# An encoder layer on one core: x split into tiles by block, w_out's tiles taking x's places one by one, and the last head's attention between the products

## The chip, the core and the metric

The kernel runs on one core of a Trainium2 chip. Its engines are TensorE (PE: matrix products, with a queue of its own for weight loads, PEld), VectorE (DVE), ScalarE (ACT), GpSimd (POOL) and SyncE (SP), which here issues every transfer. Each engine takes its instructions in a fixed order; one that waits holds up all behind it on that engine. The metric is device time in microseconds (us) of one execution, as the median of several runs; lower is better.

## What is computed

One layer of a bidirectional encoder runs over two requests, a prompt of 1024 tokens and a sample of 256, each with 16 learned meta tokens ahead:

```python
u = rms_norm(h, norm_w) @ w_in                      # 2048 -> 6656
qa, ka, va, za, qb, kb, vb, zb = split(u)           # heads of 128
ya = global_gqa(rope(norm(qa)), rope(norm(ka)), va) * silu(za)          # 8 heads, 2 kv heads
yb = neighbourhood_attention(norm(qb), norm(kb), vb, rpb) * silu(zb)    # 8 heads
out = h + concat(ya, yb) @ w_out                    # 2048 -> 2048; meta tokens dropped
```

Neighbourhood attention gives each token of a 64-wide grid the 16 meta tokens and a window of 8 x 16 tokens, with a relative bias. Inputs and outputs are 32-bit floats.

## The kernel before

**Precision.** A 32-bit product is made of three matmuls of a shorter format (fp32r): high x high, high x low, low x high. Each operand is split for that by a cast on ACT (L61, the high part) and a subtraction on DVE (L62, the low part). A split therefore costs one instruction on each of the two engines, and DVE's waits for ACT's.

**Projection.** `strips` (L176) makes u in 52 strips of 128 columns. Tokens are worked in two chunks: chunk 1 has 512 tokens (meta, sample, 240 of the prompt), chunk 2 the other 784 of the prompt in blocks of 512 and 272. A strip goes over the 2048 inputs in 4 parts of 4 tiles (WCH = 4); in each part over the blocks, and in each block over the 4 tiles, with the three matmuls at L210, L211 and L212. Weights come as raw tiles (wr, pool "raw") and are split into wh and wl (pool "w", four places each). `load_all_x` loads and splits x for chunk 2 into 16 tiles of 1584 columns, each with the parts of both blocks in it (XLAY). They lie where chunk 1's x tiles were, so a load waits until the last chunk-1 strip has passed the tiles that it covers; the loads go in an order (3, 4, 0, 1, 2, 5 ...) that follows these places.

**Attention.** The 8 global heads go first. The 8 neighbourhood heads are attended in 32 blocks, four to a head; block 4h+b is block b of head h. A block's steps in `attend_strip` (L416) are: scores on PE (L438, L272, L273), a maximum over DVE and POOL (L452, L455, L282, L284), exponentials, the meta tokens' weights Pm (L294), sums over POOL (L299, L301), the attention product on PE (L467, L470; its result is po), then y = product x gate / sum on DVE (L310, L311, L314, L318) and a write of y to device memory (yd, L319). Blocks 0 to 27 are spread between the late strips, which are the k, q, z and v strip of each neighbourhood head in turn, in the list at L836 to L843. The last head's tiles are loaded when block 27 is done (`load(7)`), and blocks 28 to 31 run at the beginning of the output products.

**Output products.** `outproj` (L979) does y @ w_out with 7 half-size products in place of 8, in passes 1, 2, 5, 6, 7, 3, 4. A pass has 5 token tiles t and 2 halves b of 512 columns: 10 steps, and 70 in all, counted here as steps 0 to 69. A step is 24 matmuls (8 tiles of k, three each; L940 to L942). Its operands are a y tile (`y_load`, `y_operand`: loaded from yd, in some passes combined with another, then split into yo, a pool of three) and 8 split w tiles (`w_load`, `w_operand`: raw tiles ww in the places of wh and wl, eight in all, split into wm, 16 places). Passes 1 and 2 read w_out itself, others sums of its quarters from device memory (td). yd[0] holds the global heads' y, yd[1] the neighbourhood heads' y, so that pass 1 needs no neighbourhood attention and pass 2 does. The pools "us", "wm" and "yo" open where the pool of x was, once that is closed behind the last strip.

**Order.** Up to step 10 a scheduler sets the order on each engine from the program's order and its own estimates, and moves loads ahead where places are free. From step 10 on, `in_order` holds each engine to the program's order. All transfers stand in one queue on SP: a load that waits for its place holds up the ones behind it.

## Time and profile before

| what | us |
|---|---|
| median of 3 runs | 2192.64 |
| lowest and highest of them | 2191.17, 2193.61 |
| the profiled execution's own time | 2193.63 |
| its span in the trace | 2191.8 |
| PE busy in the span | 2165.2 (99%) |
| DVE, ACT, POOL busy | 1646.2, 1124.4, 518.2 |
| PE's share of the chain that ended last | 94% |

The page of the profile lists busy time by engine, then the span in 40 slices with the granted clock of TensorE, the chain of waits that ended last, the costliest groups of instructions with the idle time before them, and the DMA issues. PE is busy nearly all the time, so the places to read are those where it is not: a listing of waits names each instruction that PE stood at and what ended the wait; a timeline of the stretch shows what ran around it; and busy time by stretches gives the granted clock (1.00 is full speed) and the share of the 16 DMA engines in use. A busy matmul at a lower clock is lost time too, though it counts as busy.

### The profile page before, as it was taken

How to read it: one execution, taken by the hardware profiler on the slowest of the kernel's cores; microseconds unless marked ns; L12 is line 12 of the kernel's file. 1: busy time of each engine (PE TensorE's matmuls, PEld its weight loads, DVE VectorE, ACT ScalarE, POOL GpSimd, SP SyncE). 2: the span in 40 equal slices, each digit the busy share in tenths (PEclk: the TensorE clock that was granted, in tenths of full speed). 3: DMA queues.
4: the chain of work that ended last, by engine and by line, in shares of the span. 5: the costliest groups of instructions: out<-in, count | busy, mean ns of one | idle time of the engine just before them, and what ended most of it. 6: DMA issues, size and time to landing. Idle time of an engine off the chain costs nothing.

```text
span 2191.8 us, 34025 instructions
## 1 busy us (share of the span) xinstructions
PE 2165.2 (99%) x11736; PEld 1881.7 (86%) x11736; DVE 1646.2 (75%) x2956; ACT 1124.4 (51%) x2259; POOL 518.2 (24%) x249
## 2 busy tenths in 40 slices
...
GB/s 297 221 196 229 280 307 303 345 275 264 129 220 143 106 108 116 106 107 143 104 111 116 98 122 188 167 139 137 133 123 134 95 235 113 221 190 125 218 228 113
DMA packets 262173, 383.82 MB, mean 175 GB/s; under 512 B 44880, under 2 KB 113136, under 8 KB 262000
## 3 DMA queue, kind: packets, MB, share of 16 engines
...
## 4 chain that ended last, share of the span: by engine, by line
PE 94%; DVE 2%; DMA 2%; ACT 1%; issue 1%; SPq 0%; POOL 0%; DVEq 0%; ACTq 0%; POOLq 0%
PE pp L210 21%; PE pp L211 21%; PE pp L212 21%; PE pq L942 6%; PE pq L941 6%; PE pq L940 6%; PE po L470 2%; PE sp L438 1%; PE sp L333 1%; PE sp L334 1%; PE sp L332 1%; PE po L374 1%; PE po L372 1%; PE po L373 1%; DMA ww<-in_w_out 0%
## 5 line engine op out<-in xcount | busy, mean ns | idle before, releaser
L210 PE MATMUL pp<-x,wh 128*128 128x512 f32 (+1 forms) x2496 | 892.4, 359 | 7.3 <-ACT wh L61 5.5
L211 PE MATMUL pp<-x,wh 128*128 128x512 f32 (+1 forms) x2496 | 888.6, 356 | 0.4 <-DVE x L159 0.4
L212 PE MATMUL pp<-x,wl 128*128 128x512 f32 (+1 forms) x2496 | 888.7, 356 | 0.0
L210 PEld LDWEIGHTS pp<-x,wh 128*128 128x128 f32 x2496 | 469.1, 188 | 71.6 <-ACT wh L61 7.0
L212 PEld LDWEIGHTS pp<-x,wl 128*128 128x128 f32 x2496 | 469.6, 188 | 60.9 <-DVE wl L62 0.7
L211 PEld LDWEIGHTS pp<-x,wh 128*128 128x128 f32 x2496 | 469.9, 188 | 59.9 <-DVE x L159 1.3
L220 POOL PARTITION_ALL_REDUCE m<-ms x78 | 225.8, 2895 | 378.2 <-ACT ms L218 333.3
L62 DVE TENSOR_TENSOR wl<-wr,wh 128x512 fp32r<-128x512 f32 (+1 forms) x290 | 213.1, 738 | 130.3 <-ACT wh L61 105.3
L61 ACT CAST wh<-wr 128x512 fp32r<-128x512 f32 (+1 forms) x290 | 174.9, 607 | 224.6 <-PE pp L211 206.7
L301 POOL PARTITION_ALL_REDUCE tot<-a x80 | 178.2, 2228 | 470.2 <-DVE a L299 455.1
L940 PE MATMUL pq<-wm,yo 128*128 128x512 f32 x560 | 222.0, 396 | 0.0
L941 PE MATMUL pq<-wm,yo 128*128 128x512 f32 x560 | 221.3, 395 | 0.0
L942 PE MATMUL pq<-wm,yo 128*128 128x512 f32 x560 | 221.0, 395 | 0.0
L284 POOL PARTITION_ALL_REDUCE ma<-m x80 | 104.6, 1307 | 423.3 <-DVE m L282 415.1
L942 PEld LDWEIGHTS pq<-wm,yo 128*128 128x128 f32 x560 | 105.5, 188 | 24.8 <-DVE yo L62 0.4
L941 PEld LDWEIGHTS pq<-wm,yo 128*128 128x128 f32 x560 | 105.6, 189 | 24.6
L940 PEld LDWEIGHTS pq<-wm,yo 128*128 128x128 f32 x560 | 105.8, 189 | 24.3
L336 ACT COPY S<-sp 128x512 f32<-128x512 f32 x136 | 78.4, 579 | 51.2 <-PE sp L334 38.9
L194 ACT CAST wh<-wr 128x512 fp32r<-128x512 f32 x132 | 81.1, 614 | 41.5 <-PE pp L211 41.4
L62 DVE TENSOR_TENSOR pl<-S,ph 128x512 fp32r<-128x512 f32 x136 | 97.9, 732 | 3.9 <-ACT ph L61 3.8
L352 DVE TENSOR_TENSOR S<-S,ma 128x512 f32<-128x512 f32 x136 | 97.1, 772 | 3.9 <-POOL ma L284 3.9
L61 ACT CAST ph<-S 128x512 fp32r<-128x512 f32 x136 | 83.2, 612 | 32.9 <-PE po L373 32.3
...
## 6 DMA issues: line engine op xcount, KB each, us to landing
wr<-in_w_in SPq DMA_DIRECT2D x414, 256.0 KB, 3.5
wld<-wl SPq DMA_DIRECT2D x132, 256.0 KB, 4.4
wl<-wld SPq DMA_DIRECT2D x132, 256.0 KB, 3.1
wq<-in_w_out SPq DMA_DIRECT2D x64, 256.0 KB, 5.2
td<-wq SPq DMA_DIRECT2D x64, 256.0 KB, 4.3
ww<-td SPq DMA_DIRECT2D x64, 256.0 KB, 4.9
yr<-yd SPq DMA_DIRECT2D x30, 512.0 KB, 5.4
ww<-in_w_out SPq DMA_DIRECT2D x48, 256.0 KB, 5.3
```

The lines of the kernel that those rows point to most:

```text
L61: self.hi = nc.scalar.copy(hi, full).ins
L62: return nc.vector.tensor_tensor(out=lo, in0=full, in1=hi.bitcast(F32), op=ALU.subtract).ins
L210: nc.tensor.matmul(p[:, :n], wh[:, k, :], xh[:, :n], start=first, stop=False)
L211: nc.tensor.matmul(p[:, :n], wh[:, k, :], xl[:, :n], start=False, stop=False)
L212: nc.tensor.matmul(p[:, :n], wl[:, k, :], xh[:, :n], start=False, stop=last)
L220: nc.gpsimd.partition_all_reduce(m2[:], ms[:], P, RED.add)
L284: nc.gpsimd.partition_all_reduce(ma[:], m1[:], P, RED.max)
L301: nc.gpsimd.partition_all_reduce(tot[:], a1[:], P, RED.add)
L352: nc.vector.tensor_tensor(out=s, in0=s, in1=mb, op=ALU.subtract)
L940: nc.tensor.matmul(ps[:], yh, wh, start=k == 0, stop=False)
L941: nc.tensor.matmul(ps[:], yh, wl, start=False, stop=False)
L942: nc.tensor.matmul(ps[:], yl, wh, start=False, stop=k == 7)
```

## The change

Six edits belong together.

1. `load_all_x` gives each of the 16 tiles of x two tiles: "xa" with the 512-token block, the same size and place as chunk 1's x tile, and "xb" (560 columns) with the 272-token block, in places of their own. The order of tiles is 0 to 15.
2. The pools of x stay open. w_out's raw tiles are loaded into places of "xb" (16), the split ones go into places of "xa" (16), each as the last strip has passed it. All 16 raw tiles of the first pass are asked for ahead of the products; of each later pass, four are asked for at each of the steps with t = 2 and t = 3.
3. y operands are made in the pool "w", as two halves of 4 k tiles each (yh in "wh", yl in "wl"). With four places of each, two y tiles are held where there were three.
4. Passes 2 and 4 load y through the pool "yr" like the other combined passes, once the attention has ended. Of the ten results that pass 1 keeps (U), eight lie in "us" and two in "raw".
5. The late strips of a head come in the order v, k, q, z (before: k, q, z, v).
6. `outproj` advances the last head's attention blocks only at steps 3 and on (`if 2 < n < 2 * NT`), so blocks 28 to 31 are asked for at steps 3 to 6 instead of 0 to 3.

```diff
@@ -30,8 +30,8 @@
 T1 = NMETA + NS + C1P
 T2 = NP - C1P
 NB = 512
-XLAY = ((0, 512, 512), (1024, 1312, 272))
-TX = 1584
+NT2 = 272
+NX = 560
 ALIGN = 128
 NH = 8
 EPS = 1e-6
@@ -145,14 +145,14 @@
 
 
         nc = self.nc
-        t = [self.x.tile([P, TX], F32R, tag="x", name="x", align_bytes=ALIGN) for _ in range(KT)]
-        for kt, i in enumerate((3, 4, 0, 1, 2, *range(5, KT))):
+        for kt in range(KT):
             w = self.nw[:, kt:kt + 1]
             self.xs[kt] = []
+            ta = self.x.tile([P, 2, NB], F32R, tag="xa", name="x", align_bytes=ALIGN)
+            tb = self.xb.tile([P, NX], F32R, tag="xb", name="xb", align_bytes=ALIGN)
             o = 0
-            for a, b, n in XLAY:
-                h, l = t[i][:, a:a + n], t[i][:, b:b + n]
-                r = l.bitcast(F32)
+            for h, l in ((ta[:, 0], ta[:, 1]), (tb[:, :NT2], tb[:, NX - NT2:])):
+                r, n = l.bitcast(F32), l.shape[1]
                 with self.tc.issue_after(self.early):
                     nc.sync.dma_start(r, self.x2d[kt][:, o:o + n])
                 nc.scalar.activation(h, r, AF.Copy, scale=w)
@@ -835,8 +835,8 @@
         kw, qw, kwb, qwb = (self.nqkw[:, i:i + 1] for i in (1, 0, 3, 2))
         late = []
         for h in range(NH):
-            late += [qk_late(KB + h, kwb, self.k2d[2 + h]), qk_late(QB_ + h, qwb, self.q2d[8 + h]),
-                     z_late(ZB + h, self.zd[8 + h]), v_rows_of(VB + h, 2 + h)]
+            late += [v_rows_of(VB + h, 2 + h), qk_late(KB + h, kwb, self.k2d[2 + h]), qk_late(QB_ + h, qwb, self.q2d[8 + h]),
+                     z_late(ZB + h, self.zd[8 + h])]
 
         def fill(n):
             for _ in range(min(n, len(late))):
@@ -884,42 +884,51 @@
             self.nc.sync.dma_start(r[:], self.yd[i][:, NT * h + t])
             return r[:]
 
-        if p in (1, 2, 4):
-            r = self.yo.tile([P, 2, 8, P], F32R, tag="yo", name="yo", align_bytes=ALIGN)
-            self.nc.sync.dma_start(r[:, 1].bitcast(F32), self.yd[p > 1][:, NT * (p == 4) + t])
-            return r
-        return [half(*x) for x in {7: [(0, 0), (0, 1)], 5: [(0, 1), (1, 1)], 6: [(0, 0)], 3: [(1, 0)]}[p]]
+        if self.yr is None:
+            los = [self.w.tile([P, WCH, P], F32R, tag="wl", name="yl") for _ in range(2)]
+            for i, l in enumerate(los):
+                self.nc.sync.dma_start(l[:].bitcast(F32), self.yd[p > 1][:, t, WCH * i:WCH * i + WCH])
+            return los
+        return [half(*x) for x in {7: [(0, 0), (0, 1)], 5: [(0, 1), (1, 1)], 6: [(0, 0)], 3: [(1, 0)], 2: [(1, 0)], 4: [(1, 1)]}[p]]
 
     def y_operand(self, p, t, r):
         nc = self.nc
-        if p in (1, 2, 4):
-            self.split(r[:, 0], r[:, 1], r[:, 1].bitcast(F32))
-            return r
-        if p == 7:
+        if len(r[0].shape) == 3 and r[0].shape[1] == WCH:
+            his, los, full = [], r, [l[:].bitcast(F32) for l in r]
+            for l, f in zip(los, full):
+                his.append(self.w.tile([P, WCH, P], F32R, tag="wh", name="yh"))
+                self.split(his[-1][:], l[:], f)
+            return his, los
+        if p in (2, 4):
+            v = r[0]
+        elif p == 7:
             v = r[0]
             nc.vector.tensor_tensor(out=v, in0=v, in1=r[1], op=ALU.subtract)
         else:
             v = self.ysum[t][:]
             a, b, op = {5: (r[0], r[-1], ALU.add), 6: (v, r[0], ALU.subtract), 3: (r[0], v, ALU.subtract)}[p]
             nc.vector.tensor_tensor(out=v, in0=a, in1=b, op=op)
-        o = self.yo.tile([P, 2, 8, P], F32R, tag="yo", name="yo", align_bytes=ALIGN)
-        self.split(o[:, 0], o[:, 1], v)
-        return o
+        his, los = [], []
+        for i in range(2):
+            his.append(self.w.tile([P, WCH, P], F32R, tag="wh", name="yh"))
+            los.append(self.w.tile([P, WCH, P], F32R, tag="wl", name="yl"))
+            self.split(his[i][:], los[i][:], v[:, WCH * i:WCH * i + WCH])
+        return his, los
 
     def w_load(self, p, j):
 
         b, k = divmod(j, 8)
         src = {1: (0, 0), 2: (8, 0), 3: (8, FH)}.get(p)
-        r = self.w.tile([P, FB], F32, tag=("wh", "wl")[j % 2], name="ww")
+        r = self.xb.tile([P, FB], F32, tag="xb", name="ww", align_bytes=ALIGN)[:]
         if src is None:
-            self.nc.sync.dma_start(r[:], self.td[p][:, k, FB * b:FB * b + FB])
+            self.nc.sync.dma_start(r, self.td[p][:, k, FB * b:FB * b + FB])
         else:
-            self.nc.sync.dma_start(r[:], self.io["w_out"][:, src[0] + k, src[1] + FB * b:][:, :FB])
+            self.nc.sync.dma_start(r, self.io["w_out"][:, src[0] + k, src[1] + FB * b:][:, :FB])
         return r
 
     def w_operand(self, r):
-        w = self.wm.tile([P, 2, FB], F32R, tag="wm", name="wm", align_bytes=ALIGN)
-        self.split(w[:, 0, :], w[:, 1, :], r[:])
+        w = self.x.tile([P, 2, FB], F32R, tag="xa", name="wm", align_bytes=ALIGN)
+        self.split(w[:, 0, :], w[:, 1, :], r)
         return w
 
     def x_load(self, p, t, b):
@@ -936,7 +945,7 @@
         ps = self.pq.tile([P, FB], F32, tag="pq", name="pq")
         for k in range(8):
             wh, wl = ws[k][:, 0, :], ws[k][:, 1, :]
-            yh, yl = y[:, 0, k, :], y[:, 1, k, :]
+            yh, yl = (a[k // WCH][:, k % WCH, :] for a in y)
             nc.tensor.matmul(ps[:], yh, wh, start=k == 0, stop=False)
             nc.tensor.matmul(ps[:], yh, wl, start=False, stop=False)
             nc.tensor.matmul(ps[:], yl, wh, start=False, stop=k == 7)
@@ -950,7 +959,7 @@
             nc.vector.tensor_tensor(out=out, in0=a, in1=b, op=op)
 
         if p == 1:
-            self.U[i] = self.us.tile([P, FB], F32, tag="u", name="u")
+            self.U[i] = (self.us if i < 8 else self.raw).tile([P, FB], F32, tag="u" if i < 8 else "raw", name="u")
             nc.scalar.copy(self.U[i][:], ps)
             return None
         if p == 5:
@@ -977,7 +986,7 @@
         self.nc.sync.dma_start(self.io["y"][:, NT * h + t, FH * c + FB * b:][:, :FB], o[:])
 
     def outproj(self, end_attention):
-        self.U, self.V = {}, {}
+        self.U, self.V, self.yr = {}, {}, None
         order = (1, 2, 5, 6, 7, 3, 4)
         N = 2 * NT * len(order)
 
@@ -1009,12 +1018,9 @@
                 ws[q, j] = self.w_operand(wr.pop((q, j)))
 
         make_y(0)
-        for j in range(8):
+        for j in range(16):
             load_w(0, j)
-        for j in range(16):
             make_w(0, j)
-            if j < 8:
-                load_w(0, 8 + j)
         traced = None
         for n in range(N):
             p, t, b = step(n)
@@ -1029,9 +1035,9 @@
             if n - 2 in out:
                 self.store(out.pop(n - 2), *step(n - 2))
             last = t == NT - 1
-            if t == NT - 2 and b == 0:
-                for j in range(8):
-                    load_w(q + 1, j)
+            if NT - 3 <= t < NT - 1:
+                for j in range(4):
+                    load_w(q + 1, 8 * (t - NT + 3) + 4 * b + j)
             if q:
                 for i in (n, n + 1, n + 2):
                     if i < N and i not in x:
@@ -1045,12 +1051,10 @@
             if last:
                 for k in range(8):
                     make_w(q + 1, 8 * b + k)
-                    if b == 0:
-                        load_w(q + 1, 8 + k)
             o = self.out_sums(p, 2 * t + b, ps, x.pop(n, None))
             if o:
                 out[n] = o
-            if n < 2 * NT:
+            if 2 < n < 2 * NT:
                 next(self.blocks, None)
             if traced:
                 traced = self.in_order(traced)
@@ -1104,18 +1108,16 @@
                     self.chunk1()
                 self.raw = raw
                 pool(es_x, "x", 16, side="right", **kw)
+                pool(es_x, "xb", 16, side="right", **kw)
                 pool(es_proj, "ev", 8, side="right", **kw)
                 for name, bufs in (("k", 1), ("v", 1), ("tab", 1), ("q", 1), ("z", 1), *work, ("y", 1), ("qf", 1)):
                     pool(es_attn, name, bufs, **kw)
                 self.chunk2()
                 es_proj.close()
-                es_x.close()
-                es_one.close()
                 es_pp.close()
                 pool(es_y, "pq", 4, space=PSUM, **kw)
 
-                for name, bufs in (("us", 2 * NT), ("wm", 16), ("yo", 3)):
-                    pool(es_late, name, bufs, side="right", **kw)
+                pool(es_late, "us", 8, side="right", **kw)
 
                 def end_attention():
                     es_attn.close()
@@ -1125,6 +1127,8 @@
 
                 self.outproj(end_attention)
                 es_late.close()
+                es_x.close()
+                es_one.close()
 
 
 def _grid(rows):
```

The order of the instructions moves with it. In the rows below, sp is a tile of scores, po a result of an attention product, pq a result of an output product, m1 a maximum, ww a raw and wm a split w tile; numbers behind a name tell tiles apart.

PE from the end of the last strip to the first output product, before:

```order
L212 MATMUL pp<-x,wl 128x272
L438 MATMUL sp<-qfull,kfull 128x128 x2
L272 MATMUL sp<-q,km 112x256
L273 MATMUL sp<-q,km 112x256
L438 MATMUL sp<-qfull,kfull 128x192 x2
L491 MATMUL tp<-ident,vt 128x128 x6
L491 MATMUL tp<-ident,vt 16x128
L438 MATMUL sp<-qfull,kfull 128x128 x2
L438 MATMUL sp<-qfull,kfull 128x192 x2
```

Two more groups of scores and block 27's product follow there, and then the first output product. In the changed kernel only the first of these groups (block 27's) stands behind the last strip, then step 0, and block 27's product stands in the middle of step 1:

```order
L951 MATMUL pq_20413<-wm_20353,yl_20286 128x512
L467 MATMUL po_20239<-Pm_270,vm3_271 128x256
L470 MATMUL po_20239<-S_20205,vw_19448 128x128 x2
L470 MATMUL po_20239<-S_20206,vw_19448 128x192 x2
L949 MATMUL pq_20413<-wm_20358,yh_20293 128x512
```

The transposes (tp) have moved between the strips; the scores of block 28 come after step 3, those of blocks 29, 30 and 31 each after one step more.

DVE around block 27's maximum (m1_20200 before, m1_20219 now), before:

```order
L452 TENSOR_TENSOR m1_20200<-S_20186,S_20187 128x256
L62 TENSOR_TENSOR q_20254<-qfull_20251,q_20254 128x1024
L62 TENSOR_TENSOR wm_20335<-ww_20298,wm_20335 128x512
L455 TENSOR_TENSOR m1_20200<-m1_20200,S_20187 128x128
L62 TENSOR_TENSOR wm_20338<-ww_20303,wm_20338 128x512
L62 TENSOR_TENSOR wm_20341<-ww_20308,wm_20341 128x512
L282 TENSOR_TENSOR m1_20200<-m1_20200,Sm_20192 16x256
```

and with the change:

```order
L62 TENSOR_TENSOR yl_20376<-yl_20376,yh_20380 128x512
L264 SCALAR_TENSOR_TENSOR za_20184<-z_20182,za_20184 128x512
L452 TENSOR_TENSOR m1_20219<-S_20205,S_20206 128x256
L318 SCALAR_TENSOR_TENSOR y_20055<-y_20055,r_20050 128x256
L62 TENSOR_TENSOR yl_20377<-yl_20377,yh_20383 128x512
L455 TENSOR_TENSOR m1_20219<-m1_20219,S_20206 128x128
L267 TENSOR_TENSOR zt_20181<-z_20182,za_20184 128x512
L259 TENSOR_TENSOR z_20193<-pp_20060,rb2_317 128x272
L282 TENSOR_TENSOR m1_20219<-m1_20219,Sm_20211 16x256
```

The splits between the maximum's parts were of w tiles and of head 7's q; now one is of the second half of y tile 1 (yl_20377). On SP that half is asked for here, behind the sixteenth w tile of pass 1 (ww_20371) and seven of pass 2:

```order
L926 DMA ww_20371<-in_w_out 128x512
L890 DMA yl_20376<-yd0_165 128x512
L926 DMA ww_20555<-in_w_out 128x512
L926 DMA ww_20557<-in_w_out 128x512
L926 DMA ww_20559<-in_w_out 128x512
L926 DMA ww_20561<-in_w_out 128x512
L926 DMA ww_20651<-in_w_out 128x512
L926 DMA ww_20653<-in_w_out 128x512
L926 DMA ww_20655<-in_w_out 128x512
L890 DMA yl_20377<-yd0_165 128x512
```

What moved: the y halves now stand among the w tiles of the next pass, one load each, where before a y tile was one load.

PE at the last attention product, block 31's, before (in step 6, pq_20757):

```order
L467 MATMUL po_20664<-Pm_270,vm3_271 128x256
L470 MATMUL po_20664<-S_20630,vw_20245 128x128 x2
L470 MATMUL po_20664<-S_20631,vw_20245 128x192 x2
L941 MATMUL pq_20757<-wm_20320,yo_20679 128x512
L942 MATMUL pq_20757<-wm_20320,yo_20679 128x512
```

and with the change (in step 11, pq_21056; step 12 is pq_21096):

```order
L470 MATMUL po_20818<-S_20784,vw_20264 128x128 x2
L470 MATMUL po_20818<-S_20785,vw_20264 128x192 x2
L949 MATMUL pq_21056<-wm_20969,yh_20926 128x512
L950 MATMUL pq_21056<-wm_20969,yh_20926 128x512
L951 MATMUL pq_21056<-wm_20969,yl_20920 128x512
L949 MATMUL pq_21056<-wm_20972,yh_20926 128x512
L950 MATMUL pq_21056<-wm_20972,yh_20926 128x512
L951 MATMUL pq_21056<-wm_20972,yl_20920 128x512
L949 MATMUL pq_21056<-wm_20975,yh_20926 128x512
L950 MATMUL pq_21056<-wm_20975,yh_20926 128x512
L951 MATMUL pq_21056<-wm_20975,yl_20920 128x512
L949 MATMUL pq_21096<-wm_20893,yh_21019 128x512
```

Its y goes to yd[1] and comes back as part of step 12's y tile (yh_21019, made of yr_21009); block 31's product has moved from five steps ahead of step 12 to nine matmuls ahead of it.

## The prediction

> **What bounds the kernel now.** I read the busy row of the page first, then busy time by stretches, then the list of what TensorE waits for, then TensorE's timeline over the one stage where it waits. The columns of the stretches are: start and end, length, busy time of PE, its weight loads, DVE, ACT and POOL (instructions in brackets), granted clock, DMA share, GB/s.
>
> ```profile
> span 2191.8 us, 34025 instructions
> PE 2165.2 (99%) x11736; PEld 1881.7 (86%) x11736; DVE 1646.2 (75%) x2956; ACT 1124.4 (51%) x2259; POOL 518.2 (24%) x249
> ...
> 600.00:610.00 10.00, 9.81 (x45) 7.68 (x43) 3.52 (x6) 3.02 (x8) 0.00 (x0) 1.00 0.38 119
> 610.00:620.00 10.00, 7.31 (x33) 4.88 (x34) 8.02 (x18) 7.78 (x20) 3.99 (x2) 1.00 0.82 250
> 620.00:630.00 10.00, 10.00 (x56) 8.76 (x57) 9.97 (x22) 9.74 (x21) 0.00 (x0) 1.00 0.97 314
> 1755.00:1765.00 10.00, 10.00 (x60) 8.98 (x59) 4.95 (x13) 2.94 (x7) 2.01 (x2) 1.00 0.53 167
> 1765.00:1790.00 25.00, 13.00 (x67) 11.52 (x66) 19.96 (x40) 16.18 (x32) 2.86 (x2) 0.73 0.87 306
> 1900.00:2000.00 100.00, 100.00 (x432) 81.09 (x431) 51.31 (x66) 32.78 (x51) 0.00 (x0) 1.00 0.49 169
> ```
>
> TensorE bounds the kernel, at 99% of the span, and the change removes no matmul. So only its idle time can move. In the products it runs 432 matmuls in 100 us, 0.2315 us each, so a step of 24 takes 5.56 us with nothing lost. Two places stand out: 610 to 620, where chunk 2 begins, and 1765 to 1790, between the last strip and the products, where PE works 13 us of 25 at a mean clock of 0.73.
>
> What it waits for from 1740 to the end (microseconds in total, times, longest), and the timeline of that place (start, duration, operation, and in brackets the idle time before it):
>
> ```profile
> PE sp L438 <- DMA qfull<-q2d: 4.0, 1, 4.0
> PE po L467 <- DVE Pm L294: 3.3, 1, 3.3
> PE sp L438 <- DVE S L443: 2.5, 1, 2.5
> PE tp L491 <- ACT vl L493: 2.2, 1, 2.2
> ```
>
> ```profile
> 1743.28 0.28 PE L467 MATMUL po<-Pm,vm 128*128 128x256 f32 x1
> ...
> 1744.36 0.53 PE L212 MATMUL pp<-x,wl 128*128 128x512 f32 x1
> ...
> 1748.30 0.61 PE L438 MATMUL sp<-qfull,kfull 128*128 128x128 f32 x4
> ...
> 1749.49 0.53 PE L210 MATMUL pp<-x,wh 128*128 128x512 f32 x1
> ...
> 1767.77 0.61 PE L438 MATMUL sp<-qfull,kfull 128*128 128x128 f32 x4
> ...
> 1771.90 0.55 PE L491 MATMUL tp<-ident,vt 128*128 128x128 f32 x3 [2.19 <-ACT vl L493]
> ...
> 1786.73 0.58 PE L467 MATMUL po<-Pm,vm 128*128 128x256 f32 x1 [3.29 <-DVE Pm L294]
> ...
> 1790.59 0.61 PE L438 MATMUL sp<-qfull,kfull 128*128 128x128 f32 x4
> ...
> 1791.27 0.40 PE L942 MATMUL pq<-wm,yo 128*128 128x512 f32 x1
> ```
>
> The last strip's work ends at 1767.77 and undisturbed products go on from 1791.27: 23.5 us. The work in between, at the full-clock prices of the same rows: three groups of scores at 1749.49 - 1748.30 = 1.19 (3.6), one attention product at 1744.36 - 1743.28 = 1.08, half a group at 1791.27 - 1790.59 = 0.68, four product matmuls 0.93, seven transposes about 0.8 (an estimate from the row with three in 0.55, latency included). That is 7.1, so **16.4 us are lost here**: 12.0 in the four waits, 4.4 in half-clock stretches and matmul latency.
>
> **The change, part by part.** *The transition goes.* Head 7's v strip now comes first of its four, so its transposes lie between strips; head 7's last four attention blocks (28 to 31) move from steps 0 to 3 to steps 3 to 6 of the products; and w_out's tiles arrive as x is used up. After the last strip PE now has one group of scores and then products. The four waits listed are gone: -16.4.
>
> *Chunk boundary.* In 610 to 620, 33 matmuls ran, in the next 10 us 56: (56 - 33)/56 x 10 = 4.1 us lost. x for chunk 2 was loaded and split only when the chunk-1 tiles came free; its 272-token block now has tiles of its own, which can come early. Bounds: 4.1 gained, 0 if the 512-token block, which still follows the old tiles, alone sets the pace. Two of the waits there are not for x and stay (the first below is 0.7 long), so I take -3.0.
>
> ```profile
> PE tp L253 <- DVE vm L62: 0.7, 1, 0.7
> ...
> PE pp L210 <- ACT x L158: 1.7, 1, 1.7
> ```
>
> *New wait 1, in step 1.* Block 27's attention product now stands in the middle of step 1. PE reaches it 1.19 + 5.56 + 2.78 = 9.6 us after the last strip (call that end zero). Its weights Pm come from DVE, and in DVE's order the maximum of block 27 stands behind the split of the second half of y tile 1. That half's load stands on SP behind the sixteenth w_out tile, whose place comes free only at zero, and seven tiles of pass 2.
>
> ```profile
> 1767.88 0.80 SPq L917 DMA_DIRECT2D ww<-in_w_out  x2
> ...
> 1782.90 5.63 SPq L917 DMA_DIRECT2D ww<-in_w_out  x7
> ```
>
> ```profile
> wr<-in_w_in SPq DMA_DIRECT2D x414, 256.0 KB, 3.5
> ```
>
> ```profile
> ww<-in_w_out SPq DMA_DIRECT2D x18, 256.0 KB, 5.8
> ```
>
> ```profile
> L62 DVE TENSOR_TENSOR wm<-ww,wm 128x512 fp32r<-128x512 f32 x16 | 10.3, 684 | 0.7 <-ACT wm L61 0.7
> L61 ACT CAST wm<-ww 128x512 fp32r<-128x512 f32 x16 | 9.3, 616 | 8.3 <-PE pp L212 6.2 <-DMA ww<-in_w_out 2.0
> ```
>
> ```profile
> 1753.44 0.40 DVE L282 TENSOR_TENSOR m<-m,Sm 16x256 f32<-16x256 f32 x1
> 1754.01 1.06 POOL L284 PARTITION_ALL_REDUCE ma<-m  x1 [9.88 <-DVE m L282]
> ...
> 1758.08 0.42 DVE L294 TENSOR_TENSOR Pm<-Sm,Pm 16x256 fp32r<-16x256 f32 x1
> ...
> 1761.62 0.42 DVE L311 SCALAR_TENSOR_TENSOR r<-tot,r 128x256 f32<-128x256 f32 x1
> 1764.20 0.42 DVE L314 TENSOR_TENSOR y<-po,z 128x256 f32<-128x256 f32 x1 [2.16 <-PE po L470]
> 1764.66 0.42 DVE L318 SCALAR_TENSOR_TENSOR y<-y,r 128x256 f32<-128x256 f32 x1
> ```
>
> An issue takes SP 0.40 alone (0.80 for two) and 0.80 in a crowd (5.63 for seven). Nine or so of them put the y load out at +3.9 to +6.5. A 256 KB transfer takes 3.5 in quiet stretches and 5.8 in the crowded window 1765 to 1800, so it lands at +7.4 to +12.3; I take +10. Then cast 0.62 and subtraction 0.68 (1.3), three DVE operations (1.3), and from the maximum's start to Pm's 1758.08 + 0.42 - 1753.44 = 5.06: Pm at about +17.7. PE waits 17.7 - 9.6 = **8.0**, between 5.5 and 10.4. The product's remaining half and step 2 are queued behind it on PE. Below nothing is excluded: a wait gives no time back.
>
> *New wait 2, before step 12.* Pass 2's second y tile needs block 31's y, the last one. Its product stands after 15 of 24 matmuls of step 11; then PE has only 9 matmuls, 2.08, before step 12. The rows of that way (the first y load is of pass 2 in the kernel before, the second is the kind that it has now, the third is the first kind in the crowded window):
>
> ```profile
> yd<-y SPq DMA_DIRECT2D x80, 128.0 KB, 2.2
> ```
>
> ```profile
> yo<-yd SPq DMA_DIRECT2D x15, 512.0 KB, 3.8
> yr<-yd SPq DMA_DIRECT2D x30, 512.0 KB, 5.4
> ```
>
> ```profile
> yo<-yd SPq DMA_DIRECT2D x3, 512.0 KB, 6.6
> ```
>
> From the product's start: product 1.08, the two DVE operations that make y and their gaps 1.1, issue and write 2.4, load 5.4, cast 0.6: 10.6, against 1.08 + 2.08 = 3.2 of work: 7.4 of wait, or 5.8 with a load of 3.8. If PE also waits for Pm, y ends 4.9 after Pm's start (sum and reciprocal end at 1762.04, 4.0 after 1758.08, then 0.9), and 0.2 + 2.2 + 6.6 + 0.6 follow: 14.5, against Pm's 0.42 and those 3.2: 10.9. DVE's order puts the last of 16 w splits ahead of that Pm, but these follow step 9, over a step and a half earlier, so I stay near the first: **8.0**. Before, block 31's product stood in step 6, with five whole steps, 28 us, ahead of step 12; the delay takes that cover away.
>
> *Clock.* A long wait also halves the clock for what follows:
>
> ```profile
> 1784.40:1791.20 6.80, 4.47 (x19) 4.18 (x20) 6.60 (x14) 5.78 (x11) 1.79 (x1) 0.58 1.04 410
> ```
>
> From 1786.73 to 1791.27, 4.54 us, PE did 1.08 + 0.93 + 0.68 = 2.69 of work: 1.85 for one wait of 3.3. Both new waits are longer, so 2 x 1.85 = **3.7**, at least nothing. (The Trainium skill, "TensorE: Matmul & The Clock Gate", Part 1, section "What's actually happening", has the clock halve after an idle window of about 3.4 us and come back after about 3.4 us of sustained work. By it a return costs half of 3.4, an estimate of 1.7, and the sum would be 0.3 lower; the wait of 3.3 above, which halved the clock, lies just under that window.)
>
> *At nothing:* the splits are the same number of operations on ACT and DVE, and DVE is busy 51 us of 100 in the products; uncovered, a w split is 0.62 + 0.68. The y operands are two tiles deep instead of three: load 5.4 and two splits of 1.3 lie under a tile's two steps, 11.1. The maxima of blocks 28 to 30 stand behind halves of y tiles whose places come free a tile earlier: for block 29, from the end of step 5, issue 0.4, load 3.5, split 1.3 and six DVE operations 2.5, 7.7 in all, against two groups of scores, a product, a step and 7 matmuls on PE, 10.6. With a load of 5.8 the cover is down to 0.6.
>
> *Sum:* 8.0 + 8.0 + 3.7 - 16.4 - 3.0 = +0.3, against the profiled execution's 2193.63: 2193.9. The median of the runs, 2192.64, lies 1.0 below that execution, so timed **2192.9**: gain and loss cancel.
>
> **Rivals.** *Waits covered: faster.* The y half lands at +7.4 or sooner and DVE is ahead, so wait 1 is 2, wait 2 its floor of 5.8, and one halving 1.85: 9.7 - 16.4 - 3.0 = -9.7, timed 2182.9. For it: issues of 0.40 and landings of 3.5 are what SP shows when it is not crowded. Against it: 306 GB/s in 1765 to 1790, and the sixteenth tile's place, which no speed of transfer frees before zero.
>
> *x's block gains nothing.* If the early 272-token loads only move traffic ahead of chunk 1's last weights, and the 512-token tiles come at the old pace (314 GB/s at 620 to 630, nearly full), the 3.0 is not earned: +3.3, timed 2195.9.
>
> *The queue decides: slower.* From a landing of the y half at +12.3 on, pass 2's loads share the transfers with every later y tile. It lands at +13.5: wait 1 is 11.5; block 29's cover is used up, 1.5; wait 2 is 10.9; the halvings 3.7: 27.6 - 19.4 = +8.2, timed 2200.8. For it: landings of 5.8 and 6.6 in the old transition. Against it: by step 11 few loads are left, and 169 GB/s is the steady rate.
>
> **How the numbers follow.** The forecast has 0.45; covered waits 0.19; no gain at the chunk 0.15; the queue 0.21. The forecast's own range is 2188 to 2199 (waits 5.5 to 10.4 and 5.8 to 10.9, chunk 0 to 4.1, not all at one end). With half of the outer cases left out: 2183 to 2201. A measurement of this kernel tells about 0.2%, 4.4 us, from no change: 2188.2 to 2197.0 is the same. Of the forecast 0.09 lies below that, 0.26 in it and 0.10 above; covered waits give 0.18 faster and 0.01 same; the chunk case 0.09 same and 0.06 slower; the queue 0.02 same and 0.19 slower. Together faster 0.27, same 0.38, slower 0.35.
>
> **What would show it.** Right: no wait for qfull, S or vl after the last strip; PE waiting about 8 us for Pm at L467 with 12 of step 1's matmuls done; about 8 at L949 of step 12 for yh; granted clock near 0.5 for some 3 us behind each; 610 to 620 with over 45 matmuls. Wrong: the first product waiting for wm (w_out late, the transition not removed), a y half landing well before +7, Pm of block 31 there long before its product, or waits in later passes from the shallower y tiles.

## The result, and the profile after

The changed kernel takes 2186.11 us (median of 6 runs, 2183.33 to 2186.95) against 2193.80 for the kernel before (6 runs, 2191.17 to 2194.68): a ratio of 0.9965, 95% interval 0.9954 to 0.9975. It is faster by 7.7 us, 0.35%; the forecast was no change, 2192.9, with a range of 2183 to 2201.

The busy row and the stretches of the changed kernel, with the same columns as in the prediction:

```profile
span 2185.0 us, 34137 instructions
PE 2158.3 (99%) x11736; PEld 1882.2 (86%) x11736; DVE 1642.2 (75%) x2991; ACT 1120.7 (51%) x2294; POOL 519.3 (24%) x249
```

```profile
600.00:610.00 10.00, 9.64 (x44) 7.52 (x42) 5.85 (x10) 4.63 (x11) 0.00 (x0) 1.00 0.44 134
610.00:620.00 10.00, 8.23 (x42) 7.34 (x43) 7.83 (x17) 5.86 (x15) 2.38 (x2) 0.83 0.78 246
620.00:630.00 10.00, 10.00 (x53) 8.62 (x52) 9.57 (x17) 9.40 (x18) 0.89 (x1) 1.00 0.93 306
...
1900.00:2000.00 100.00, 100.00 (x443) 82.81 (x442) 52.77 (x77) 33.91 (x62) 0.00 (x0) 1.00 0.48 169
```

The last row is the surprise. At the same granted clock and with PE busy all the time in both, it holds 443 matmuls where the kernel before had 432. A product matmul takes 0.2267 us instead of 0.2320 (median distance from one start to the next; the mean before is 0.2324): over the 1680 of them, 9 to 10 us.

What PE waits for from 1740 on, and the places in PE's timeline:

```profile
PE pq L949 <- ACT yh L61: 5.1, 1, 5.1
PE pq L949 <- DVE z L259: 5.0, 1, 5.0
```

```profile
1773.27 0.53 PE L949 MATMUL pq<-wm,yh 128*128 128x512 f32 x1
...
1784.01 0.77 PE L949 MATMUL pq<-wm,yh 128*128 128x512 f32 x1 [4.98 <-DVE z L259]
...
1789.26 0.32 PE L467 MATMUL po<-Pm,vm 128*128 128x256 f32 x1
...
1854.77 0.28 PE L467 MATMUL po<-Pm,vm 128*128 128x256 f32 x1
...
1863.32 0.79 PE L949 MATMUL pq<-wm,yh 128*128 128x512 f32 x1 [5.13 <-ACT yh L61]
```

The four waits of the old transition are gone; products begin at 1773.27, one group of scores after the strip. Two waits have come in their place, at step 1 and at step 12. The granted clock halves behind both (stretches of the two waits and of the work after them):

```profile
1778.70:1784.00 5.30, 0.32 (x2) 0.03 (x1) 5.30 (x13) 1.26 (x3) 0.00 (x0) 0.86 1.04 374
1784.00:1790.40 6.40, 6.39 (x22) 5.24 (x22) 4.10 (x11) 3.31 (x9) 2.91 (x2) 0.59 0.94 311
...
1858.10:1863.30 5.20, 0.09 (x1) 0.00 (x0) 0.00 (x0) 0.65 (x2) 0.00 (x0) 0.78 0.67 215
1863.30:1868.00 4.70, 4.68 (x11) 3.64 (x12) 4.52 (x8) 1.63 (x3) 0.00 (x0) 0.52 0.88 307
```

To see where the time went I take, for each matmul of a trace, the distance to the next one's start, subtract the settled distance for its width (0.2267 us for 512 columns, 0.220 for 496, 0.125 for 272, 0.119 for 256, 0.162 for 192, 0.109 for 128), and sum by stretch. This is the loss of PE against one fixed pace:

| stretch, us | what runs there | lost before | lost changed |
|---|---|---|---|
| 0 to 590 | start, chunk 1 | 16.4 | 16.3 |
| 590 to 640 | chunk 2 begins | 5.6 | 4.5 |
| 640 to 1740 | chunk 2's strips, attention | 4.5 | 9.3 |
| 1740 to 1763 | chunk 2's last strips | 0.1 | 0.1 |
| 1763 to 1800 | last strip, transition | 16.3 | 7.9 |
| 1800 to 1880 | products, last attention blocks | 1.9 | 7.8 |
| 1880 to the end | products | 7.7 | 0.0 |

Sum of the differences before rounding: -6.7, against spans of 2191.8 and 2185.0, -6.8. Some 9.5 us of what the kernel before lost in the last two rows is pace. Without that gain the change would be 2 to 3 us slower, where the forecast had +0.3 for all that it saw. That these two lie so close is partly luck: the forecast took 19.7 us for the two new waits and their clock, which cost 15.2, and nothing for the 4.8 in the strips.

### The profile page after: what moved, and what is told of

The parts are those of the page before. It is cut to its first block, busy times and chain, and to the rows that moved or that the text cites. A ratio compares the mean times of both kernels' runs of the same rounds, so it can differ in the third digit from the quotient of the medians.

```text
span 2185.0 us, 34137 instructions
## 1 busy us (share of the span) xinstructions
PE 2158.3 (99%) x11736; PEld 1882.2 (86%) x11736; DVE 1642.2 (75%) x2991; ACT 1120.7 (51%) x2294; POOL 519.3 (24%) x249
## 4 chain that ended last, share of the span: by engine, by line
PE 92%; DVE 3%; DMA 2%; ACT 1%; SPq 1%; issue 1%; POOL 0%; DVEq 0%; ACTq 0%; POOLq 0%
PE pp L210 20%; PE pp L212 20%; PE pp L211 20%; PE pq L949 6%; PE pq L951 6%; PE pq L950 6%; PE sp L438 2%; PE po L470 2%; PE sp L334 1%; PE sp L333 1%; PE sp L332 1%; PE po L372 1%; PE po L373 1%; PE po L374 1%; SPq L227 0%
## 5 line engine op out<-in xcount | busy, mean ns | idle before, releaser
L210 PE MATMUL pp<-x,wh 128*128 128x512 f32 (+1 forms) x1664 | 654.1, 394 | 7.0 <-ACT wh L61 6.5
L212 PE MATMUL pp<-x,wl 128*128 128x512 f32 (+1 forms) x1664 | 649.4, 391 | 0.2 <-DVE wl L62 0.2
L211 PE MATMUL pp<-x,wh 128*128 128x512 f32 (+1 forms) x1664 | 649.4, 391 | 0.0
L210 PEld LDWEIGHTS pp<-x,wh 128*128 128x128 f32 x1664 | 313.3, 188 | 63.7 <-ACT wh L61 7.7
L212 PEld LDWEIGHTS pp<-x,wl 128*128 128x128 f32 x1664 | 313.0, 188 | 62.4 <-DVE wl L62 1.4
L211 PEld LDWEIGHTS pp<-x,wh 128*128 128x128 f32 x1664 | 313.5, 188 | 52.1
L211 PE MATMUL pp<-xb,wh 128*128 128x272 f32 x832 | 241.8, 291 | 0.0
L210 PE MATMUL pp<-xb,wh 128*128 128x272 f32 x832 | 240.4, 289 | 0.0
L212 PE MATMUL pp<-xb,wl 128*128 128x272 f32 x832 | 239.8, 288 | 0.0
L949 PE MATMUL pq<-wm,yh 128*128 128x512 f32 x560 | 221.1, 395 | 10.1 <-ACT yh L61 5.1
L950 PE MATMUL pq<-wm,yh 128*128 128x512 f32 x560 | 219.7, 392 | 0.0
L951 PE MATMUL pq<-wm,yl 128*128 128x512 f32 x560 | 219.7, 392 | 0.0
L210 PEld LDWEIGHTS pp<-xb,wh 128*128 128x128 f32 x832 | 157.0, 189 | 7.3
L211 PEld LDWEIGHTS pp<-xb,wh 128*128 128x128 f32 x832 | 156.9, 189 | 7.2
L212 PEld LDWEIGHTS pp<-xb,wl 128*128 128x128 f32 x832 | 157.8, 190 | 0.1
```

What stands on the lines that cost most here:

```text
L210: nc.tensor.matmul(p[:, :n], wh[:, k, :], xh[:, :n], start=first, stop=False)
L211: nc.tensor.matmul(p[:, :n], wh[:, k, :], xl[:, :n], start=False, stop=False)
L212: nc.tensor.matmul(p[:, :n], wl[:, k, :], xh[:, :n], start=False, stop=last)
L949: nc.tensor.matmul(ps[:], yh, wh, start=k == 0, stop=False)
L950: nc.tensor.matmul(ps[:], yh, wl, start=False, stop=False)
L951: nc.tensor.matmul(ps[:], yl, wh, start=False, stop=k == 7)
```

## The experiments

All ratios below are against the kernel before, measured beside each experiment on the same chip.

**Is it the place of y?** The change puts y low. The first run puts the changed kernel's y operands high again; to make room for them, U (16 KB) changes places with them.

```diff
-  los = [self.w.tile([P, WCH, P], F32R, tag="wl", name="yl") for _ in range(2)]
+  los = [self.yp.tile([P, WCH, P], F32R, tag="yl", name="yl") for _ in range(2)]
...
-  self.U[i] = (self.us if i < 8 else self.raw).tile([P, FB], F32, tag="u" if i < 8 else "raw", name="u")
+  self.U[i] = (self.w if i < 8 else self.raw).tile([P, FB], F32, tag=("wh", "wl")[i % 2] if i < 8 else "raw", name="u")
```

> The changed kernel with one thing undone: the split y operands lie at 104 to 120 KB of each partition (a pool of their own) and the results U that pass 1 keeps take their places in the low pool at 11 to 27 KB. Same number and layout of tiles, same matmuls. Theory A (the place of the stationary operand sets the pace of the product matmuls): from 1900 to 2000 us TensorE runs about 432 matmuls as before, not 443, and the kernel is about 9 us slower than the changed one, near 2195. Rival B (the pace comes from elsewhere, from w tiles in x's places or from y in two halves): still 443 and about 2186.

Measured 2207.60, ratio 1.0062 (1.0047 to 1.0078), and this stretch:

```profile
1900.00:2000.00 100.00, 100.00 (x430) 80.13 (x429) 50.36 (x73) 32.64 (x59) 0.00 (x0) 1.00 0.59 209
```

430 matmuls: the pace is lost, as theory A says. The rest of the 21 us over the changed kernel is mainly a longer transition, with a wait of 13.1 for block 27's Pm:

```profile
PE po L467 <- DVE Pm L294: 13.1, 1, 13.1
```

The new places of y are ones that the strips' results hold until then, which may be why; that wasn't tested.

The second run does the opposite, y low in the kernel before.

```diff
-  r = self.w.tile([P, FB], F32, tag=("wh", "wl")[j % 2], name="ww")
+  r = self.wr2.tile([P, FB], F32, tag="ww", name="ww")
...
+  his.append(self.w.tile([P, WCH, P], F32R, tag="wh", name="yh"))
...
-  for name, bufs in (("us", 2 * NT), ("wm", 16), ("yo", 3)):
+  for name, bufs in (("us", 2 * NT), ("wm", 16), ("wr2", 8)):
```

> The kernel before with one part of the change alone: y operands in the low pool in two halves (passes 2 and 4 through yr), and w_out's raw tiles, which lay there, in a pool of eight where the y operands were. x, the late order, the attention's steps and the w loads stay as before. Theory A: 443 matmuls in 1900 to 2000 us instead of 432, the transition from strips to products loses its 16 us as before, and the time is about 9 us under the kernel before, near 2185. Rival B: 432, near 2194.

Measured 2186.71, ratio 0.9969 (0.9958 to 0.9981), nearly what theory A asks for, but not for its reason:

```profile
1900.00:2000.00 100.00, 100.00 (x432) 81.08 (x431) 48.71 (x68) 28.85 (x51) 0.00 (x0) 1.00 0.47 164
```

The pace has not moved. The time comes from the transition, where the loss falls from 16.3 to 9.7: the first product comes 3.6 us after the last strip's last matmul instead of 21.3. The raw w tiles have places of their own there, which is the likely reason; the run does not separate it from y's new places. Low y is not the cause of the pace, and a matching time alone would have hidden it. Theory A falls.

**A map of places.** Bursts of 48 product-like matmuls behind the last store, with the operands at 24 places each.

```diff
+  for i in range(n):
+      burst(T[i][:, :P], T[n - 1][:, 1024:1536])
+  for i in range(n):
+      burst(low, T[i][:, 1024:1536])
...
```

> The changed kernel with bursts of 48 matmuls (128x128 stationary, 128x512 moving, like the products) behind its last store; the output is the same. First both operands vary alone: stationary at 15 KB and then at 24 places from 30 to 218 KB with the moving operand at 222 KB; then the stationary at 15 KB and the moving operand at 24 places; then the stationary at 24 places with the moving one at 34 KB. Theory A with a threshold: 0.2265 us a matmul up to some place of the stationary operand between 27 and 104 KB, 0.232 beyond it, and no effect of the moving one. Theory A with a slope: it grows evenly from 0.2265 to about 0.236. Rival C (two operands collide only when both lie in the same half): slow only where both are high or both low. Rival D (it needs other engines and transfers at work): 0.2265 everywhere here.

Two bursts of PE's timeline, with the two outermost tiles, 188 KB apart, in either role:

```profile
2230.97 11.14 PE L1079 MATMUL bp<-atx,ata 128*128 128x512 f32 x48
...
3029.17 11.18 PE L1079 MATMUL bp<-ata,atx 128*128 128x512 f32 x48
```

All 72 full-clock bursts last 11.14 to 11.18 us; inside each, after the first few, the distance is 0.226 to 0.227. The place makes no difference, so theory A falls in both forms, and rival C too; rival D is left. But all these tiles, unlike w's before, start on multiples of 256 bytes. In the built programs (start in a partition, in bytes): before, y started at 118528 = 463 x 256 and w at 143232 = 559.5 x 256; in the changed kernel 11008 = 43 x 256 and 157440 = 615 x 256; with y high, 104000 = 406.25 x 256.

**Start on 256 bytes.** Two numbers in the kernel before.

```diff
-  w = self.wm.tile([P, 2, FB], F32R, tag="wm", name="wm", align_bytes=ALIGN)
+  w = self.wm.tile([P, 2, FB], F32R, tag="wm", name="wm", align_bytes=256)
...
-  r = self.yo.tile([P, 2, 8, P], F32R, tag="yo", name="yo", align_bytes=ALIGN)
+  r = self.yo.tile([P, 2, 8, P], F32R, tag="yo", name="yo", align_bytes=256)
```

> The kernel before with one number changed twice: the split w tiles and the split y tiles start on multiples of 256 bytes (w at 143104 instead of 143232 bytes of the partition, y at 118272 instead of 118528); nothing else moves. Theory A2 (a moving or stationary operand that does not start on a multiple of 256 bytes makes a product matmul slower; before, w's tiles started 128 bytes off, in the changed kernel and nowhere else do all operands of the products start on 256): 443 product matmuls in 1900 to 2000 us instead of 432, and about 9 us less than the kernel before, near 2184. Rival E (it is the distance between w and y or the number of bytes between pools): 432 and near 2193.

Measured 2183.97, ratio 0.9957 (0.9945 to 0.9970):

```profile
1900.00:2000.00 100.00, 100.00 (x443) 82.80 (x442) 51.33 (x65) 29.64 (x45) 0.00 (x0) 1.00 0.50 173
```

The changed kernel's pace, and 9.7 us, more than the whole change, with w 128 bytes lower and y 256. The transition stays as it was (15.1 us lost). This run alone does not say whether each start counts or their distance; the next does, with starts moved by 0 to 64 words of 4 bytes.

```diff
+  s = T[16 + (r == 2)][:, P * k + so:P * k + so + P]
+  w = T[k][:, FB * (r == 1) + mo:FB * (r == 1) + mo + FB]
+  nc.tensor.matmul(ps[:], s, w, start=i == 0, stop=i == N - 1)
...
```

> The changed kernel with bursts of 96 matmuls behind its last store, in the products' pattern (y high on w high, y high on w low, y low on w high, over 8 k tiles); the output is the same. Bursts are named by which operand starts how many 4-byte words past a multiple of 256 bytes: moving 0, 8, 16, 32, 48, 64; stationary 8, 16, 32, 48, 64; both 32; and one with the same two operands all the time. Theory A2: 96 x 0.2265 = 21.7 us where both offsets are 0 or 64, 96 x 0.232 = 22.3 with 32 on the moving side, about as much or more (0.2335) with 16 on the stationary side. Rival: no difference between offsets; then the earlier pace was not alignment alone.

20 us inside the bursts with nothing moved, w moved by 8, 16 and 32 words, y by 48, and both by 32:

```profile
2567.50:2587.50 20.00, 20.00 (x90) 16.55 (x89) 0.00 (x0) 0.00 (x0) 0.00 (x0) 1.00 0.00 1
2590.00:2610.00 20.00, 20.00 (x87) 16.09 (x86) 0.00 (x0) 0.00 (x0) 0.00 (x0) 1.00 0.00 1
2612.50:2632.50 20.00, 20.00 (x89) 16.42 (x88) 0.00 (x0) 0.00 (x0) 0.00 (x0) 1.00 0.00 0
2635.00:2655.00 20.00, 20.00 (x87) 16.20 (x86) 0.00 (x0) 0.00 (x0) 0.00 (x0) 1.00 0.00 1
...
2770.00:2790.00 20.00, 20.00 (x89) 16.41 (x88) 0.00 (x0) 0.00 (x0) 0.00 (x0) 1.00 0.00 1
...
2815.00:2835.00 20.00, 20.00 (x90) 16.53 (x89) 0.00 (x0) 0.00 (x0) 0.00 (x0) 1.00 0.00 1
```

Here w is the moving and y the stationary operand. The mean distance over a whole burst of 96, first starts included, tells it finer:

| w moved by | y moved by | w minus y, modulo 256 bytes | us per matmul |
|---|---|---|---|
| 0 | 0 | 0 | 0.2281 |
| 32 bytes | 0 | 32 | 0.2345 |
| 64 | 0 | 64 | 0.2301 |
| 0 | 192 | 64 | 0.2301 |
| 128 | 0 | 128 | 0.2334 |
| 0 | 128 | 128 | 0.2334 |
| 192 | 0 | 192 | 0.2344 |
| 0 | 64 | 192 | 0.2344 |
| 0 | 32 | 224 | 0.2344 |
| 256 | 0 | 0 | 0.2285 |
| 0 | 256 | 0 | 0.2281 |
| 128 | 128 | 0 | 0.2281 |

Rows with the same distance agree within 0.0004, and both operands moved by 128 bytes cost nothing. Over the last 60 distances of a burst, where it has settled, the means are 0.2267 at 0, 0.2289 at 64, 0.2323 at 128 and 0.2333 at 32, 192 and 224. So theory A2 was right that the offset matters and wrong in what is measured: it is the distance of the moving from the stationary operand modulo 256 bytes, not either one's start. The kernels agree with the settled figures: distance 128 before and with y low in it (0.2324 in both), 0 in the changed one and with starts on 256 (0.2267), 192 with y high (0.2333). No other engine works during these bursts, so rival D falls: contention is not needed. Why PE cares isn't shown.

**Wait 2: the blocks one step earlier.**

```diff
-            if 2 < n < 2 * NT:
+            if 1 < n < 2 * NT:
```

> The changed kernel with the last head's attention blocks asked for one step earlier, at steps 2 to 5. Theory (wait 2 is the way of block 31's y back to step 12): block 31's product comes a step or so earlier, 5.4 us, so the 5.1 us wait for yh at step 12 and its half clock, 7.5 us in all, fall to 2 or less, and the time is 2179 to 2182. Rival (the DVE backlog after the strip sets block 31's end, whatever step it is asked for at): wait 2 stays over 4 us, or as much comes back as a wait for scores before step 3, and the time stays at 2186.

Measured 2179.17, ratio 0.9933 (0.9921 to 0.9946), 7 us under the changed kernel, as the theory has it. Of PE's waits from 1740 on, the one for yh is gone, and nothing came back for it before step 3:

```profile
PE pq L949 <- DVE z L259: 4.4, 1, 4.4
PE po L467 <- DVE Pm L294: 0.4, 1, 0.4
```

Another step earlier gives no more:

```diff
-            if 2 < n < 2 * NT:
+            if 0 < n < 2 * NT:
```

> The changed kernel with the attention's blocks asked for at steps 1 to 4. Wait 2 has no more to give (none was left with steps 2 to 5), and the loads of head 7 are no earlier, so block 28's scores come ahead of step 2 and may wait for qfull, as before. Expected 2179 to 2183; under 2177 only if wait 1 (block 27 and the z strip's eviction on DVE) shrinks too, for which nothing speaks.

Measured 2180.75, ratio 0.9940 (0.9927 to 0.9952): same as the run before within their intervals, wait 1 unchanged at 4.5.

**Wait 1: a late y half, or DVE's backlog?** The next run keeps y tile 1's splits behind block 27's Pm (on top of blocks 2 to 5).

```diff
+            if n == 0:
+                with self.tc.issue_after(self.pma), self.tc.issue_after(self.pmd):
+                    make_y(1)
...
```

> The kernel with the attention's blocks at steps 2 to 5, and the splits of y tile 1 queued on ACT and DVE behind block 27's Pm. Theory A as in the prediction (the late landing of y tile 1's second half holds block 27's chain up): Pm comes up to 5 us earlier, the wait at step 1 (4.4 us and a half clock, 6.7 together) falls to 2 or less, time about 2174. Rival B (DVE is busy without a gap, the landing only coincides): Pm comes earlier by the two subtractions alone, 1.3 us, time 2177 to 2179.

Measured 2180.28, ratio 0.9933 (0.9920 to 0.9945), no gain. PE's waits there:

```profile
PE pq L949 <- DVE z L259: 3.2, 1, 3.2
PE po L467 <- DVE Pm L294: 2.0, 1, 2.0
```

Pm comes 15.1 us after the last strip's end. In the kernel that this run builds on it came after 16.2 (16.8 in the changed kernel), so the two subtractions are worth 1.1, near rival B's 1.3 and far from the up to 5 of theory A. The wait only divides itself between two places, and the clock stayed halved for 6.8 us where it had for 3.4; the median lies 1.3 over rival B's range, which the interval of the ratio takes in. Theory A falls, and rival B fits DVE's rows: in the changed kernel DVE runs from 1766 to block 27's maximum at 1783.78 with no gap over 0.3 us, so the y half's landing only coincides. Taking work from DVE was meant to confirm it:

```diff
+            self.nc.gpsimd.tensor_tensor(out=w[:, 1, :], in0=r, in1=w[:, 0, :].bitcast(F32), op=ALU.subtract)
...
```

> As the run before it, and every second of the 16 first w splits has its subtraction on POOL instead of DVE. Rival B: DVE's queue is shorter by 8 x 0.64 = 5.1 us, block 27's Pm comes that much earlier, the wait at step 1 falls by 3 to 5 us, time about 2174. Theory A: nothing more than the run before it gave; and if POOL's subtractions take over 2 us each, w tiles come late and step 0 or 1 waits for wm.

Measured 2206.30, ratio 1.0054 (1.0040 to 1.0068). It neither confirms nor refutes rival B: POOL, in its own order, holds these splits behind its all-reduces and takes twice DVE's time for one. So no run shortened DVE's backlog, and rival B rests on DVE's rows and on the run before.

```profile
L933 POOL TENSOR_TENSOR wm<-ww,wm 128x512 fp32r<-128x512 f32 x8 | 12.0, 1525 | 16.3 <-DMA q2d<-rs_r 9.4 <-ACT za L263 6.9
```

**The late strips' order and x in two tiles.** The changed kernel lost 4.8 us more in 640 to 1740. Three orders of a head's late strips were tried on the kernel with blocks at steps 2 to 5 (the first is shown here), and the first edit alone on the kernel before.

```diff
-            late += [v_rows_of(VB + h, 2 + h), qk_late(KB + h, kwb, self.k2d[2 + h]), qk_late(QB_ + h, qwb, self.q2d[8 + h]),
-                     z_late(ZB + h, self.zd[8 + h])]
+            late += [qk_late(KB + h, kwb, self.k2d[2 + h]), qk_late(QB_ + h, qwb, self.q2d[8 + h]),
+                     z_late(ZB + h, self.zd[8 + h]), v_rows_of(VB + h, 2 + h)]
```

> The kernel with the attention's blocks at steps 2 to 5, with the late strips of a head back in the order k, q, z, v. The changed kernel lost 9.3 us against a pace of 0.2267 us in 640 to 1740 us, the kernel before 4.5. Theory L (the new order costs that, its loads of v wait): the loss falls back to about 4.5; at the end head 7's transposes stand behind the last strip again with a wait of 1 to 2 us; sum about 3 us less, near 2176. Rival X (x in two tiles costs it): it stays at 9, and the time is 2179 to 2182.

> The kernel with the attention's blocks at steps 2 to 5 and the late strips in the order k, q, v, z. Theory P (the 5 us wait at step 1 is for the bank of the last z strip, emptied by DVE behind its backlog): with z still last the wait stays at 4 to 5 us. Theory L on the strips (v ahead of k makes scores wait for v's loads): with k and q ahead the 2.4 us of waits in 640 to 1740 go, and the transposes stay between strips; about 2176 to 2177, at best 2175.

> As the run before it with the order k, z, v, q, so that the last strip is q's, whose PSUM banks are emptied at the end of a longer chain (square, sum over POOL, reciprocal, product on DVE) than z's one operation. Theory P: the wait at the start of step 1 is then for q's banks (rs_r on DVE) and grows from 4.4 to 6 us or more, and block 28's scores may wait for the late q: 2179 or more. Rival Q (the w tiles of step 1 set the wait, and z's eviction only ends last by chance): the wait stays as long or gets shorter, and the time is 2177 or less.

With k, q, z, v: 2176.83, ratio 0.9922 (0.9908 to 0.9935). With k, q, v, z: 2177.56, 0.9926 (0.9913 to 0.9938). With k, z, v, q: 2193.57, 0.9997 (0.9988 to 1.0006). The first two lose 6.7 and 6.9 us in 640 to 1740 instead of 9.3, not the 4.5 that theory L asked for. The waits in that stretch fall from 2.4, by the account of losses, to 0.0 and 0.6: theory L holds for these. The changed kernel's (their idle time alone):

```profile
PE sm_ps L272 <- DVE mx L342: 1.1, 2, 0.6
PE sp L438 <- DMA vw<-vn: 0.9, 1, 0.9
```

At the end, k, q, z, v has a wait of 6.5 for the transposes, more than the 1 to 2 expected, and the transition loses 9.3 instead of 7.0, so that the gain over the kernel it builds on is 2.3 us:

```profile
PE tp L491 <- DVE vt L246: 6.5, 1, 6.5
```

With k, q, v, z, theory P forecast a wait of 4 to 5 for z's bank; it is 3.8 in two parts, and 2.8 for Pm comes on top:

```profile
PE pq L949 <- DVE z L259: 3.8, 2, 2.1
PE po L467 <- DVE Pm L294: 2.8, 1, 2.8
```

With q last PE does not stand at the products' banks but at block 27:

```profile
PE po L467 <- DVE Pm L294: 16.8, 1, 16.8
```

The order of the engines changed too much there for the run to tell theory P from rival Q; it shows that this order costs the whole gain. The changed kernel itself decides between them, in the part on wait 1 below.

```diff
-        t = [self.x.tile([P, TX], F32R, tag="x", name="x", align_bytes=ALIGN) for _ in range(KT)]
...
+            ta = self.x.tile([P, 2, NB], F32R, tag="xa", name="x", align_bytes=ALIGN)
+            tb = self.xb.tile([P, NX], F32R, tag="xb", name="xb", align_bytes=ALIGN)
...
```

> The kernel before with the first edit alone: x in two tiles, the rest as before (w tiles of the products 128 bytes off, old transition). As the prediction has it, the start of chunk 2 gains 3 us: 2190. As the changed kernel's trace has it, it gains about 1 (lost time in 590 to 640 us 5.6 before, 4.5 changed). Theory L: nothing more in 640 to 1740, so about 2192.5. Rival X: 4 to 5 us more there, about 2197.

Measured 2195.78, ratio 1.0006 (0.9997 to 1.0015): no change. The beginning of chunk 2 loses 4.5 instead of 5.6, and 640 to 1740 loses 7.3 instead of 4.5, of which 0.6 are single waits and the rest (6.7 against 4.5) is spread over the strips' matmuls. So the first edit gains 1 and costs about 3: rival X holds for the spread part. The spread part lies in the strips' 512-column matmuls (against 0.2267 us each, 10.1 lost before and 12.1 here), whose operands stand at distance 0 modulo 256 bytes in both kernels. So the rule found above does not explain it, and what slows those matmuls by 1 ns isn't settled. Nor does the rule show in the 272-column matmuls: the first edit moves the high part of their x from distance 0 to 128, and they lose 2.8 in both.

**Both findings on the kernel before.** The kernel with y low and w's raw tiles in a pool of their own, and one number more:

```diff
-  w = self.wm.tile([P, 2, FB], F32R, tag="wm", name="wm", align_bytes=ALIGN)
+  w = self.wm.tile([P, 2, FB], F32R, tag="wm", name="wm", align_bytes=256)
```

> The kernel before with y operands low and the raw tiles in a pool of eight (which gave 6.7 us, in the transition), and w's split tiles on a multiple of 256 bytes. If pace and transition are independent, 443 matmuls in 1900 to 2000 us and 2193.5 - 6.7 - 9.7 = about 2177. If one takes away from the other, more than 2180.

Measured 2177.03, ratio 0.9923 (0.9911 to 0.9936), with 443 matmuls in 1900 to 2000: the two add up. Beside the order k, q, z, v above (2176.83) this kernel is the fastest measured, some 9 us under the changed kernel, and it needs neither x in two tiles nor the attention moved.

## Why the prediction was wrong

**The step that failed** is the first one: "the change removes no matmul. So only its idle time can move." It took 0.2315 us as what a product matmul costs (the 432 take in those that the stretch's edges cut; the distance is 0.2324) and used it for both kernels; that edits 2 and 3 give w and y other starts was costed at nothing. The runs show 0.2324 against 0.2267 for the same matmul, as the distance of its operands modulo 256 bytes goes from 128 to 0: some -9.5 us, which no row of waits or of busy time can show, since PE counts as busy in both. It is edit 2 that does it, by putting the split w tiles on multiples of 256 bytes; y started on one in both kernels, and y low alone left the pace at 0.2324. The strips of the kernel before had 0.227 as the median distance of the same 128x512 matmul; two paces for one shape in one trace was the sign.

**The transition goes: right.** -16.4 in the sum, 16.3 by the account above, and its four waits are gone.

**Wait 1: over a quarter too large, and wrong in its place and cause.** Forecast 8.0 for Pm and 1.85 for the clock; lost 7.7 in all, and none of it at L467. PE stands at the beginning of step 1, for a PSUM bank of the z strip that DVE empties (L259), and half-clocked work covers the rest, so PE reaches block 27's product just as Pm is ready. In the built program step 1's result has the very bank of the z strip's 272-token result, and the last of the 16 w splits (first DVE row below) ended 4 us before PE went on at 1784.01: theory P, not rival Q. SP and DVE there:

```profile
1771.30 4.34 SPq L926 DMA_DIRECT2D ww<-in_w_out  x7
1775.97 0.33 SPq L890 DMA_DIRECT2D yl<-yd  x1
```

```profile
1779.21 0.68 DVE L62 TENSOR_TENSOR wm<-ww,wm 128x512 fp32r<-128x512 f32 x1
...
1782.02 0.68 DVE L62 TENSOR_TENSOR yl<-yl,yh 128x512 fp32r<-128x512 f32 x1
...
1783.43 0.43 DVE L259 TENSOR_TENSOR z<-pp,rb 128x272 f32<-128x272 f32 x1
1783.78 0.40 DVE L282 TENSOR_TENSOR m<-m,Sm 16x256 f32<-16x256 f32 x1
...
1788.42 0.41 DVE L294 TENSOR_TENSOR Pm<-Sm,Pm 16x256 fp32r<-16x256 f32 x1
```

The y half left SP 3.9 us after the strip's end (1772.08) and was split at +9.9, Pm came at +16.8 where +17.7 was forecast. ACT's cast did wait 2.8 us for the half's landing at 1781.24, but DVE was not idle ahead of the split, and with the split out of the way the wait stayed: by these rows the backlog of 16 w splits, four y splits, the strip's evacuation and block 27 sets it. Pm's time was forecast nearly right for a wrong reason, which is luck.

**Wait 2: right, a third too large.** Forecast 8.0 and 1.85; it waited 5.1 and lost 7.5 with the clock. The way from block 31's y to the cast of yh:

```profile
1856.64 0.42 DVE L318 SCALAR_TENSOR_TENSOR y<-y,r 128x256 f32<-128x256 f32 x1
1857.09 0.37 SPq L319 DMA_DIRECT2D yd<-y  x1
1859.20 0.33 SPq L884 DMA_DIRECT2D yr<-yd  x1
...
1862.65 1.14 ACT L61 CAST yh<-yr 128x512 fp32r<-128x512 f32 x2 [7.60 <-DMA yr<-yd]
```

The load took some 3.4 us from 1859.20, like the 3.8 of the floor and not the 5.4 of the row that was chosen. One step earlier for the blocks removed it all.

**Clock: halved as forecast, but at a higher price.** Both waits halved it, at 2.7 and 2.4 us by the rows (7.7 - 5.0 and 7.5 - 5.1) where 1.85 was put in. The 1.85 was read off a wait of 3.3 (1783.4 to 1786.7) in the kernel before which had not halved the clock; it was at half from that wait's beginning on:

```profile
1779.60:1781.80 2.20, 0.00 (x0) 0.00 (x0) 2.20 (x6) 0.75 (x3) 0.57 (x1) 0.94 1.03 394
1781.80:1783.80 2.00, 1.58 (x10) 1.30 (x10) 1.97 (x4) 1.91 (x4) 0.49 (x1) 0.87 1.07 348
1784.00:1786.70 2.70, 0.00 (x0) 0.00 (x0) 2.65 (x6) 2.27 (x7) 0.00 (x0) 0.50 1.04 416
```

So half of that slow stretch (1783.3 to 1790.1) passed while PE stood anyway. In the changed kernel more of it falls on work: by the clocks of 0.59 over 6.4 us and 0.52 over 4.7, some 5.3 and 4.5 us. In the Trainium skill's terms ("TensorE: Matmul & The Clock Gate", Part 1, "What's actually happening") both waits, 5.0 and 5.1, lie past the 3.4 us window, and the trace agrees. The 3.4 us of sustained work until the clock returns, from which the prediction took its other estimate of 1.7, are less than the 5.3 and 4.5 us here; the measurement decides.

**The chunk boundary: too large.** Forecast -3.0, measured -1.1 in both kernels with x in two tiles. The waits for x fell from 2.1 us (1.7 and 0.4) to 0.5, but the one for vm at L253 grew from 0.7 to 1.6, and 610 to 620 held 42 matmuls, not over 45, and ran at a clock of 0.83 where it had been 1.00. That halving was put at nothing, and the size goes with it: of the traces with x in two tiles, those with a halved clock there lost 4.1 to 6.1 us in 590 to 640, and the four without (k, q, z, v; k, q, v, z; k, z, v, q; y tile 1 behind) 2.8 to 3.2, against 5.1 to 5.6 with x in one tile: a gain of some 2 to 3, not far from the forecast. Why the clock halves in some of them is not shown.

**Unforeseen:** +4.8 in the strips, half of it waits from v ahead of k and q, half of it from x in two tiles, which the prediction's "nothing" for other stages had not looked at.

Of the rivals, none had the pace. The time came near the "waits covered" case (2182.9) by luck, since no wait was covered.
